# A DiT block's weights in two parts: the low parts of 28 input-weight tiles by a negated copy on ScalarE and an adding transfer

## The chip, the core and the metric

The kernel runs on one core of one Trainium2 chip. The time is device time in microseconds for one execution. Engines: PE is TensorE (PEld its weight loads), DVE is VectorE, ACT is ScalarE, POOL is GpSimd, SP is SyncE, which here only issues DMAs. A line number L234 is line 234 of the kernel before.

## What is computed

Two layers over 256 latent and 256 context tokens of width 1024, all in float32. Each layer is a half FFN, a mixer (attention in the first layer, a bidirectional mLSTM in the second) and another half FFN; every part has its own modulation (shift, scale, gate from a vector per stream) and a post-norm:

```
def half_ffn(h, shift, scale, gate, w_in, w_out, g, b):
    xm = modulate(h, shift, scale)
    a, u = jnp.split(xm @ w_in, 2, axis=-1)
    y = (jax.nn.silu(a) * u) @ w_out
    return post_norm(h, 0.5 * gate * y, g, b)
```

`w_in` is 1024 x 5632 and `w_out` 2816 x 1024. The modulation vectors are `silu(c) @ ada_w[i] + ada_b[i]`, nine chunks of 1024 per layer and stream. There are four half FFNs: the first and second belong to layer 0, the third and fourth to layer 1.

## The kernel before, in words

**Two-part products.** A matmul in full float32 is replaced by three in a reduced form (`fp32r`): each operand is kept as a rounded high part h and the rest, l = x - h, and `mm3` (L232) adds wh*xh, wh*xl and wl*xh in PSUM. Every weight tile is therefore split after it is loaded. `chunk` (L211) does that for a 128 x 1024 tile: `raw` (L197) loads it by a DMA from SP into one of three buffers (`RAW`), `pair` (L206) takes one of seven buffers (`WB`) that hold h and l side by side, and `split` (L217) writes h by a cast on ACT (L218) and l by a subtraction on DVE (L223). The subtraction goes in four pieces while `self.fine` is set. A pair is free again when TensorE has used it, so the cast of a tile waits for TensorE; a raw buffer is free when the subtraction has read it.

**An FFN's order.** `ffn` (L645) works in two halves of 11 hidden units. A unit (`unit_in`, L657) is two weight tiles, 48 matmuls on 512 columns (both token streams together), then the Silu on ACT (L558), the product with the other half on DVE (L559), and a split of the result. Then `unit_out` (L668) multiplies the 11 units by output weights for eight blocks of the width, and the second half follows.

- In the second and third FFN the first half begins with four leading units (`LEAD`), whose weights are kept and used once for the latent and once for the context tokens, while the norm before them is still running. Units 4 to 10 then stream, two tiles each: 14 tiles per FFN, and they are the tiles that the change touches. `fine` is set until unit 6 is emitted.
- Their second halves use another scheme (`fast_in`, L593), which forms sums of weight quarters on DVE; `fast_sums` (L566) makes the sums of the inputs during the output blocks of the first half.
- The first FFN has its own start and no fast half; the fourth has its own function.

**Work on the side.** The modulation vectors of later parts are made on DVE (`ada_dot`, L324 to L327) from tiles of `ada_w` in two buffers (`ada_load`, L317), which SP loads. A few of these products are emitted after each unit (`DOTS`: four behind an input unit, three behind an output block). Each engine works off its own queue in order; the order within a queue comes from a scheduler over the emitted program, apart from instructions that are pinned (`pin`). The residual's scaling (L533 on DVE, L534 on ACT) is emitted behind each unit too. GpSimd does small parts of the norms (L454, L491).

**DMA queues.** All loads are issued from SP. The program reserves 512 bytes per partition for descriptors of transfers that GpSimd issues:

```
nc = _bacc.Bacc("TRN2", target_bir_lowering=False, num_devices=1, dynamic_dma_scratch_size=512)
```

Of the kernel before, what the change touches and what calls it, by code (L numbers as in the profile page):

```python
# [13 lines left out]
AF = mybir.ActivationFunctionType  # L14
ALU = mybir.AluOpType
# [116 lines left out]
def part_k(part, k):  # L132
    return k // 4 * 8 + part * 4 + k % 4


class Stream:


    def __init__(self, b, chunks, sh=0):
        self.b, self.chunks, self.kept = b, chunks, (None, None)  # L140
        self.sh = sh if callable(sh) else lambda c: sh
# [24 lines left out]
class Body:  # L166
    def __init__(self, ctx, tc, a, out):
        self.tc, self.nc, self.a, self.out = tc, tc.nc, a, out
        self.n = 0
        self.sp = ctx.enter_context(tc.tile_pool(name="sp", bufs=1))  # L170
        self.pp = ctx.enter_context(tc.tile_pool(name="pp", bufs=1, space=PSUM))
        self.later, self.running = [], []
        self.fence = {}
        self.fine = False

        self.nraw, self.spare = 0, None


    def t(self, shape, dt=F32, tag=None, bufs=None, pool=None):
# [31 lines left out]
    def chunk(self, src, sh=0):  # L211
        r = self.raw(src)
        h, l = self.pair(sh=sh)
        self.split(r, h, l)
        return h, l

    def split(self, x, h, l):  # L217
# [427 lines left out]
    def ffn(self, layer, s, gate, groups, side, start=None, cpool=None):  # L645
        nc, V = self.nc, self.nc.vector
        li = layer * 2 + s
        allg = BOTH
        call = lambda *k: side.get(k, lambda: None)()
        with self.tc.tile_pool(name=f"ffn{li}", bufs=1) as gp:  # L650
            self.gp, self.gt, self.gw, self.gn = gp, {}, T, NFH
            done = 0
            if start:
                start(self)
                done = NSTART

            def unit_in(j, w, g, steps={}, ks=range(ND), ps=None):  # L657
                n = g[1] - g[0]
                pa, pu = ps or (self.mm(), self.mm())
                for k in ks:  # L660
                    for part, o in ((0, pa), (1, pu)):
                        self.mm3(o[:, :n], w(part_k(part, k)), self.x(k, g), k == 0, k == ND - 1)
                    self.steps(steps.get((j, k), ""))
                if ks[-1] < ND - 1:
                    return pa, pu
                self.ffn_g(j, pa, pu, g)

            def unit_out(hf, d, w, g, steps={}):  # L668
                t0, t1 = g
                y = self.mm()  # L670
                for i in range(NFH):
                    gh, gl = self.gt[hf * NFH + i]
                    self.mm3(y[:, : t1 - t0], w(d * NFH + i), (gh[:, t0:t1], gl[:, t0:t1]), i == 0, i == NFH - 1)
                    self.steps(steps.get((int(g == CTX), d - (ND - TAIL), i), ""))
                for gg in groups:
                    if gg[0] >= t0 and gg[1] <= t1:
                        v = 0 if gg[0] == 0 else 1
                        z = self.h[:, d, gg[0] : gg[1]]
                        V.scalar_tensor_tensor(z, y[:, gg[0] - t0 : gg[1] - t0], gate()[:, v, d : d + 1], z, ALU.mult, ALU.add)  # L679
                        if hf:  # L680
                            self.add_sum(gg, d)

            w_in, w_out = self.a["ffn_in"][li], self.a["ffn_out"][li]
            stream = lambda j: Stream(self, [w_in[2 * j + i] for i in range(2)])
            for hf in range(2):
                js = list(range(hf * NFH, (hf + 1) * NFH))[0 if hf else done :]
                if hf == 0 and not start:
                    first = js[:LEAD]
                    ws = {j: Keep(self, [w_in[2 * j + i] for i in range(2)], SH) for j in first}
                    assert len(self.running) == 1  # L690

                    k0, k1 = range(ND // 2), range(ND // 2, ND)
                    for j in first[:-1]:
                        unit_in(j, ws[j], LAT, LEADSTEP[li])
                    j = first[-1]
                    ps = unit_in(j, ws[j], LAT, ks=k0)
                    assert not self.running
                    pc = unit_in(first[0], ws[first[0]], CTX, ks=k0)
                    ws[j](ND)
                    unit_in(first[0], ws[first[0]], CTX, ks=k1, ps=pc)  # L700
                    unit_in(j, ws[j], LAT, ks=k1, ps=ps)
                    for j in first[1:]:
                        unit_in(j, ws[j], CTX)
                    for j in first:
                        call("in", j)
                    js = js[LEAD:]
                fast = cpool is not None and hf == 1
                for j in js:
                    if fast:
                        self.fast_in(j, w_in, st)  # L710
                        continue
                    unit_in(j, stream(j), allg)
                    assert not self.running
                    if j >= LEAD + FAFTER:
                        self.fine = False
                    call("in", j)
                    self.residual(2, self.pin)
                if not hf:
                    self.residual(len(self.later))
                w = Stream(self, [w_out[hf * NFH + i] for i in range(NFH)])  # L720
                body = ND - TAIL if hf else ND
                if fast:
                    more.close()
                for d in range(body):
                    if cpool and not hf and d == SUMSAT:
                        cpool.close()
                        self.n += 1
                        more = ExitStack()
                        st = more.enter_context(self.tc.tile_pool(name=f"st{self.n}", bufs=1, side="right"))
                        self.fast_operands(st)  # L730
                    unit_out(hf, d, w, allg)
                    if cpool and not hf and d >= SUMSAT and d - SUMSAT < 2:
                        self.fast_sums(d - SUMSAT)
                    call("out", hf, d)
                if body < ND:
                    w = Keep(self, w.chunks, SH, w)
                    self.fine = True
                    for g in groups:
                        for d in range(body, ND):
                            unit_out(hf, d, w, g, TAILSTEP)  # L740
                    self.steps('B')
# [975 lines left out]
```

## Time and profile before

| What | Value |
|---|---|
| Runs (3), median | 1662.06 us (1657.20 to 1662.81) |
| The profiled execution | 1661.01 us, span 1659.1 us |
| Mean granted TensorE clock | 0.992 |
| Busy share PE / PEld / DVE / ACT / POOL | 98% / 88% / 82% / 45% / 4% |
| Read from HBM | 248.76 MB, 151 GB/s over the span |
| Streamed units of the second FFN's first half | about 611 to 687 us |
| Streamed units of the third FFN's first half | about 967 to 1043 us |

Rows of a timeline read: start, length, engine, line, operation, output <- inputs, shapes, count; in brackets the idle time of the engine just before and what ended it. A row of waits reads: who waited, for whom, microseconds in total, times, longest. A row of stretches gives for each engine the busy time and the number of instructions (PE, PEld, DVE, ACT, POOL), then the granted clock, the DMA engines' mean busy share and GB/s. Matmuls are pipelined, so a busy PE is not PE at its peak.

### The profile page before, as it was taken

To read this page: it belongs to the slowest core of one execution; us is meant where nothing else is said; L and a number is where in the kernel's file an instruction comes from. 1 tells how busy PE (TensorE), PEld (TensorE's weight loads), DVE (VectorE), ACT (ScalarE), POOL (GpSimd) and SP (SyncE) were. 2 spreads that over 40 slices of the span, in tenths; PEclk is the share of its full clock that TensorE was granted. 3 is DMA by queue.
4 is the path that set the end of the run, shared out by engine and by line. 5 is a ranking of instruction groups with operands and counts; after the bars stand their busy time and mean duration, and the time that the engine had idled before them with its cause. 6 is when DMAs were issued, how large, how long until landed. Compare 5 with 4: busy or idle time off the path is not lost. (4 is left out here: it accounts for less than half of the span.)

```text
span 1659.1 us, 26570 instructions
## 1 busy us (share of the span) xinstructions
PE 1624.8 (98%) x10308; PEld 1463.5 (88%) x10308; DVE 1354.8 (82%) x2689; ACT 743.6 (45%) x1267; POOL 62.3 (4%) x76
## 2 busy tenths in 40 slices
PE   9999999999989999999999999899999999999998
PEld 6888888899978998889999988689999989999987
DVE  5899977749898979999965888779975967897687
ACT  5532132314765443325652424215651566656542
POOL 0000000001010200000000100000000100020000
PEclk9999999999999999999999999898999999999999
DMA  9577766622203157733352267743351342438552
GB/s 372 188 234 234 246 203 193 200 64 84 64 1 113 54 158 223 218 113 117 113 179 69 84 203 251 256 126 103 127 153 55 111 134 78 128 115 253 179 178 89
DMA packets 72207, 251.54 MB, mean 152 GB/s; under 512 B 7952, under 2 KB 10768, under 8 KB 72080
## 3 DMA queue, kind: packets, MB, share of 16 engines
q1 hardware_dynamic: 71504, 249.05, 47.3%
q8 instruction: 81, 1.33, 0.3%
q10 hardware_dynamic: 576, 0.79, 0.1%
q14 instruction: 46, 0.38, 0.1%
HBM read 248.76 MB, written 1.05 MB: 151 GB/s over the span
## 5 line engine op out<-in xcount | busy, mean ns | idle before, releaser
L234 PE MATMUL t<-t,t 128*128 128x256 f32 (+2 forms) x8412 | 1332.6, 320 | 19.3 <-ACT t L218 15.1
L234 PEld LDWEIGHTS t<-t,t 128*128 128x128 f32 x8412 | 1199.4, 189 | 140.1 <-ACT t L218 17.6
L218 ACT CAST t<-t 128x1024 fp32r<-128x1024 f32 (+3 forms) x521 | 428.4, 843 | 481.7 <-PE t L234 233.4
L223 DVE TENSOR_TENSOR t<-t,t 128x256 fp32r<-128x256 f32 (+2 forms) x740 | 513.6, 728 | 116.9 <-ACT t L218 113.2
L327 DVE SCALAR_TENSOR_TENSOR t<-t,t 128x1024 bf16<-128x1024 f32 x224 | 263.8, 1221 | 28.2 <-DMA t<-in_ada_w 27.3
L894 PE MATMUL t<-t,t 128*128 128x256 f32 (+1 forms) x256 | 79.4, 310 | 0.0
L896 PE MATMUL t<-t,t 128*128 128x256 f32 (+1 forms) x256 | 78.7, 307 | 0.0
L895 PE MATMUL t<-t,t 128*128 128x256 f32 (+1 forms) x256 | 78.4, 306 | 0.0
L558 ACT ACTIVATE t<-t 128x512 f32<-128x512 f32 (+1 forms) x71 | 34.3, 488 | 95.4 <-PE t L234 95.3
L679 DVE SCALAR_TENSOR_TENSOR t<-t,t,t 128x256 f32<-128x256 f32 x96 | 42.6, 478 | 41.6 <-PE t L234 41.6
L559 DVE TENSOR_TENSOR t<-t,t 128x512 f32<-128x512 f32 (+1 forms) x71 | 38.9, 552 | 34.4 <-PE t L234 28.0
L454 POOL TENSOR_TENSOR t<-t,t 128x256 f32<-128x256 f32 x30 | 23.5, 785 | 1142.2 <-ACT t L444 1140.9
L1409 PE MATMUL t<-t,t 128*128 128x512 f32 (+3 forms) x286 | 60.2, 366 | 1.9 <-ACT t L1486 1.0
L822 PE MATMUL t<-t,t 128*128 128x512 f32 (+1 forms) x300 | 60.5, 364 | 0.0
L1409 PEld LDWEIGHTS t<-t,t 128*128 128x128 f32 (+2 forms) x286 | 43.8, 159 | 18.3 <-issue 2.3
L822 PEld LDWEIGHTS t<-t,t 128*128 128x128 f32 x300 | 51.5, 189 | 8.9
L444 ACT ACTIVATE t<-t 128x256 f32<-128x256 f32 x72 | 26.1, 411 | 72.0 <-DVE t L437 72.0
L534 ACT ACTIVATE t<-t,t 128x256 f32<-128x256 f32 x64 | 29.4, 503 | 56.6 <-DVE t L533 56.5
L894 PEld LDWEIGHTS t<-t,t 128*128 128x128 f32 x256 | 48.3, 189 | 2.6
L895 PEld LDWEIGHTS t<-t,t 128*128 128x128 f32 x256 | 48.2, 188 | 2.6
L896 PEld LDWEIGHTS t<-t,t 128*128 128x128 f32 x256 | 48.1, 188 | 2.5
L602 DVE TENSOR_TENSOR t<-t,t 128x512 f32<-128x512 f32 x66 | 45.3, 686 | 0.6
(200 smaller groups left out, 1066.3 us busy)
## 6 DMA issues: line engine op xcount, KB each, us to landing
t<-in_ffn_in SPq DMA_DIRECT2D x168, 512.0 KB, 4.0
t<-in_ada_w SPq DMA_DIRECT2D x137, 512.0 KB, 4.3
t<-in_ffn_out SPq DMA_DIRECT2D x66, 512.0 KB, 4.3
t<-in_ffn_last SPq DMA_DIRECT2D x22, 512.0 KB, 3.6
t<-in_att_in SPq DMA_DIRECT2D x12, 512.0 KB, 3.5
t<-in_att_out SPq DMA_DIRECT2D x8, 512.0 KB, 3.5
t<-in_ml_qk SPq DMA_DIRECT2D x8, 512.0 KB, 3.6
t<-in_ml_v SPq DMA_DIRECT2D x8, 512.0 KB, 3.6
```

The lines of the kernel that those rows point to most:

```text
L218: self.behind(self.nc.scalar.copy(h, x))
L223: self.behind(self.nc.vector.tensor_tensor(out=ls, in0=xs, in1=hs.bitcast(F32), op=ALU.subtract))
L234: mm = lambda *k, **kw: self.nc.tensor.matmul(*k, skip_group_check=not group, **kw)
L327: ins = nc.vector.scalar_tensor_tensor(self.tmp().bitcast(BF16), r, 1.0, self.cb[:, v, :], ALU.mult, ALU.mult, accum_out=to)
L559: V.tensor_tensor(out=sl, in0=sl, in1=pu[:, :n], op=ALU.mult)
L602: add = lambda o, x, y: V.tensor_tensor(out=o, in0=x, in1=y, op=ALU.add)
L679: V.scalar_tensor_tensor(z, y[:, gg[0] - t0 : gg[1] - t0], gate()[:, v, d : d + 1], z, ALU.mult, ALU.add)
L822: pin(nc.tensor.matmul(o, gs[g], ws[k][w][:, i : i + n], start=k == k0 and g == w == 0, stop=k == k1 - 1 and g == 1,))
L894: mm(o, self.xh[:, k, c], wh, start=k == 0, stop=False)
L895: mm(o, self.xh[:, k, c], wl, start=False, stop=False)
L896: mm(o, self.xl[:, k, c], wh, start=False, stop=k == ND - 1)
L1409: mm = lambda *k, **kw: pin(nc.tensor.matmul(*k, **kw))
```

## The change

For the 14 streamed tiles of the second FFN's first half and the 14 of the third's, the low part is made in another way. ACT casts the tile to h as before, then writes the negated tile, rounded to the same reduced form, into l. Then GpSimd issues a DMA that reads the weights from HBM a second time and adds them to what stands in l, which leaves x - h. DVE takes no part. All other splits stay.

```
@@ Body.__init__
+        self.added = False
@@ def chunk(self, src, sh=0):
         r = self.raw(src)
         h, l = self.pair(sh=sh)
-        self.split(r, h, l)
+        if self.added:
+            self.behind(self.nc.scalar.copy(h, r))
+            self.nc.scalar.activation(l, r, AF.Copy, scale=-1.0)
+            self.nc.gpsimd.dma_start(l, src, accum_op=ALU.add)
+        else:
+            self.split(r, h, l)
         return h, l
@@ ffn, for j in js:
+                    self.added = cpool is not None
                     unit_in(j, stream(j), allg)
+                    self.added = False
```

`cpool` is given for the second and third FFN alone, and their second halves leave this loop before these lines.

## The prediction

> **What bounds the kernel now.** I read the page's busy times first, then TensorE's waits, then the two stages that the change touches.
>
> The page's first part:
>
> ```profile
> span 1659.1 us, 26570 instructions
> ...
> PE 1624.8 (98%) x10308; PEld 1463.5 (88%) x10308; DVE 1354.8 (82%) x2689; ACT 743.6 (45%) x1267; POOL 62.3 (4%) x76
> ```
>
> TensorE is busy for 1624.8 of 1659.1 us, so at most 34 us can be won by removing waits alone. The profiled execution took 1661.01 us, 1.05 us below the median of the runs (1662.06), inside their spread of 1657.20 to 1662.81; sums below are made against 1661.0. About 0.3% (5.0 us) is what a measurement of this kernel can tell from no change.
>
> TensorE's own waits (line waited for: us in total, times, longest):
>
> ```profile
> PE t L234 <- ACT t L218: 15.1, 6, 8.2
> PE t L234 <- DVE t L223: 2.0, 4, 1.2
> ```
>
> Half of it is one wait of 8.2 us. The PE timeline and the stretches around it (busy time by engine, granted clock, DMA share, GB/s) show where:
>
> ```profile
> 1059.67 58.63 PE L234 MATMUL t<-t,t 128*128 128x512 f32 x259 [8.20 <-ACT t L218]
> 1119.85 0.39 PE L234 MATMUL t<-t,t 128*128 128x256 f32 x1 [1.55 <-ACT t L218]
> 1120.58 1.44 PE L234 MATMUL t<-t,t 128*128 128x256 f32 x5 [0.35 <-DVE t L223]
> 1124.25 11.03 PE L234 MATMUL t<-t,t 128*128 128x256 f32 x65 [2.23 <-ACT t L218]
> ```
>
> ```profile
> 611.00:687.00 76.00, 76.00 (x337) 62.98 (x336) 72.88 (x123) 25.97 (x38) 0.00 (x0) 1.00 0.73 222
> ...
> 967.00:1043.40 76.40, 76.40 (x341) 63.33 (x340) 66.86 (x112) 24.61 (x35) 0.00 (x0) 1.00 0.77 247
> 1051.50:1059.70 8.20, 0.03 (x1) 0.03 (x1) 5.63 (x9) 1.52 (x3) 0.00 (x0) 0.75 0.84 275
> 1059.70:1065.90 6.20, 6.20 (x15) 4.85 (x16) 4.17 (x8) 0.23 (x1) 0.00 (x0) 0.50 0.80 258
> 1124.30:1130.70 6.40, 6.36 (x28) 6.07 (x29) 5.32 (x6) 3.30 (x6) 0.00 (x0) 0.50 0.41 160
> ```
>
> The two 76 us stretches are the changed units of the second and the third FFN: TensorE has no gap in either, GpSimd (the fifth pair of numbers) does nothing, and the DMA engines are already 0.73 and 0.77 busy. The 8.2 us wait stands behind the third FFN's stretch, at 1051.5; then the clock is granted at 0.50 for 6.2 us, which loses 3.1 us, and 4.1 us of waits (1.55 + 0.35 + 2.23) with 6.4 us at half clock (3.2 us) follow at 1118. So the third FFN holds 8.2 + 3.1 + 4.1 + 3.2 = 18.6 us that are lost to late operands; the second FFN holds nothing.
>
> Why the wait at 1051.5? DVE's timeline through that stage:
>
> ```profile
> 976.75 1.23 DVE L327 SCALAR_TENSOR_TENSOR t<-t,t 128x1024 bf16<-128x1024 f32 x1 [0.95 <-DMA t<-in_ada_w]
> ...
> 982.91 1.22 DVE L327 SCALAR_TENSOR_TENSOR t<-t,t 128x1024 bf16<-128x1024 f32 x1
> ...
> 990.11 1.23 DVE L327 SCALAR_TENSOR_TENSOR t<-t,t 128x1024 bf16<-128x1024 f32 x1 [1.17 <-DMA t<-in_ada_w]
> ...
> 1004.75 1.22 DVE L327 SCALAR_TENSOR_TENSOR t<-t,t 128x1024 bf16<-128x1024 f32 x1
> ...
> 1054.07 1.22 DVE L327 SCALAR_TENSOR_TENSOR t<-t,t 128x1024 bf16<-128x1024 f32 x1 [1.52 <-DMA t<-in_ada_w]
> ...
> 1058.29 0.68 DVE L559 TENSOR_TENSOR t<-t,t 128x512 f32<-128x512 f32 x1
> ```
>
> The last unit's gate product (L559) waits in DVE's queue until 1058.29 behind the modulation products (L327). Those have two load buffers, so a buffer's round is its products plus a reload: SP issues one as soon as the products are done (below, 979.15, for the products at 982.91: 3.76 us). Rounds take (1004.75 - 976.75) / 4 = 7.0 us, and the reload is what most of them wait for, the subtractions only partly.
>
> **Part one: the 28 DVE subtractions that go.** One form per row:
>
> ```profile
> L218 ACT CAST t<-t 128x1024 fp32r<-128x1024 f32 x309 | 322.9, 1050 | 359.5 <-PE t L234 217.2 <-issue 68.0 <-DMA t<-in_ffn_out 23.4
> L223 DVE TENSOR_TENSOR t<-t,t 128x1024 fp32r<-128x1024 f32 x236 | 286.9, 1222 | 67.6 <-ACT t L218 64.8 <-PE t L234 1.5
> L223 DVE TENSOR_TENSOR t<-t,t 128x256 fp32r<-128x256 f32 x350 | 133.8, 426 | 43.0 <-ACT t L218 42.8
> ```
>
> Fourteen tiles per FFN: units 4 to 6 are subtracted in four pieces, 7 to 10 whole. That is 12 x 4 x 0.426 + 16 x 1.222 = 40.0 us of DVE. In the second FFN nothing waits for it, so it is worth 0 there. In the third, two 1.22 us products and a reload of 4.3 us (below) bound a round at 6.7 us, against 7.0 now: over the six rounds between 970 and 1016, some 2 us, at most 3 with the earlier start of the first product.
>
> **Part two: ScalarE.** Its timeline at the first changed tile of each FFN (the cast), and at the Silus of the leading units (L558), behind the last of which TensorE's next work is that tile:
>
> ```profile
> 592.15 1.04 ACT L218 CAST t<-t 128x1024 fp32r<-128x1024 f32 x1
> ...
> 605.25 0.38 ACT L558 ACTIVATE t<-t 128x256 f32<-128x256 f32 x1 [1.41 <-PE t L234]
> ...
> 610.67 0.38 ACT L558 ACTIVATE t<-t 128x256 f32<-128x256 f32 x1 [1.39 <-PE t L234]
> ```
>
> ```profile
> 947.61 1.35 ACT L218 CAST t<-t 128x1024 fp32r<-128x1024 f32 x2
> ...
> 967.10 0.38 ACT L558 ACTIVATE t<-t 128x256 f32<-128x256 f32 x1 [1.48 <-PE t L234]
> ```
>
> 28 negations; no such instruction stands in the trace, the nearest is the cast of the same tile, 1.05 us: 29.4 us. ACT is busy 25.97 of 76.00 us in the stretch, so 14.7 more fit. They are tightest beside the leading units, whose Silus are 610.67 - 605.25 = 5.4 us apart with two tiles between them: 2 x 2.10 + 0.38 + a small cast (1.35 - 1.05 = 0.3 by the row at 947.61) = 4.9 us. I cost it at 0; were that cover gone, it would be 1.05 us per tile, behind which the next cast is queued. The raw buffer is now freed by ACT, not by DVE, so SP's weight loads go out earlier, and in the order of instructions some modulation loads stand one place later on SP.
>
> **Part three: the 28 transfers.** GpSimd has nothing before them and nothing but the next transfer waits behind one in either stretch. But a tile's low half is complete only when its transfer has landed, so TensorE now waits for the DMA, and behind its waiting matmul stand the rest of the in-order stream and the Silu and gate product that follow from it. TensorE's own order stays but for two matmuls. What time there is for that comes out of ACT's rows above.
>
> Second FFN: cast ends at 593.2, negation at 594.2, first use at 610.7. A tile lasts 24 matmuls x 76.00 / 337 = 5.41 us, so the fourteenth is wanted at 610.7 + 13 x 5.41 = 681.0. Third FFN: ready at 950.0, fourteenth wanted at 967.3 + 70.3 = 1037.6. If each transfer takes T and they go one after the other, the fourteenth lands 14 T after the first is ready, and TensorE starts to wait from T = 86.8 / 14 = 6.2 us on (6.26 in the third).
>
> No GpSimd transfer is in the trace. The rows that bound T (queue; then KB each, median us to landing):
>
> ```profile
> q1 hardware_dynamic: 71504, 249.05, 47.3%
> ...
> t<-in_ffn_in SPq DMA_DIRECT2D x168, 512.0 KB, 4.0
> t<-in_ada_w SPq DMA_DIRECT2D x137, 512.0 KB, 4.3
> ...
> t<-in_att_in SPq DMA_DIRECT2D x12, 512.0 KB, 3.5
> ...
> t<-in_start_in SPq DMA_DIRECT2D x1, 512.0 KB, 9.9
> ```
>
> ```profile
> 975.83 0.33 SPq L203 DMA_DIRECT2D t<-in_ffn_in  x1
> 979.15 2.94 SPq L321 DMA_DIRECT2D t<-in_ada_w  x2
> ```
>
> A packet costs an engine 0.473 x 1659.1 x 16 / 71504 = 0.176 us; a 512 KB load is 8 of 4 KB per engine, 1.40 us, so 2.1 of the fastest landing (3.5) are fixed. An accumulation reads the weights and the tile: 16 reads, 2.81 us. Where SP's queue has the engines 0.72 of the time and takes turns, that is 2.81 x 1.72 = 4.8 us. With 2.1 fixed and 0.33 for the issue (SP's row at 975.83; GpSimd's own is not in the trace): **T = 7.3 us**. Bounds: 3.5, if it is no dearer than a plain load on idle engines, and 9.9, the slowest 512 KB load here, in full traffic.
>
> Do they overlap one another? By the Trainium skill, DMA: Bandwidth & Descriptors, section "The descriptor swizzle", a transfer to 128 partitions takes nine read descriptors per engine, and Collectives: The Full Stack, "The bandwidth ceiling", gives an add two reads, so 17; of 16 bytes each, the kernel's 512 bytes of ring hold 32, so an estimate from these pages is that a second one doesn't fit beside the first. No run here shows it. The rows alone lead near: 0.73 busy plus 2.81 / 5.41 = 0.52 is 1.25 of the engines, so even overlapping transfers would only keep a pace of 5.41 x 1.25 = 6.8 us if SP's queue gave nothing up. I take one after the other.
>
> The same DMA page, "Anatomy of one DMA", puts a GpSimd transfer at about 2.0 us plus its bytes at 436 GB/s; for a megabyte read that is an estimate of 4.4 us, by which the sum would be the hidden case below. The rows speak for more, since 1.40 us of transport lands after 4.0 to 4.3 here.
>
> **The sum.** Second FFN: 14 x 7.3 - 86.8 = 15.4 us later. Third FFN: 14 x 7.3 - 87.6 = 14.6 us later, but this fills the 18.6 us that TensorE loses there anyway; what is then late is the modulation chain. Its reloads share the engines: up to 1.4 us more in each of six rounds, +8.4, against the gain of at most 3; I take +2.5, near the middle. Total +17.9: 1661.0 + 17.9 = **1679 us**.
>
> **Rivals.**
> *Transfers far slower* (T 8.5 to 9.9 and above): the loaded row at 9.9 and DVE's 0.96 busy share beside GpSimd speak for it, the unloaded 3.5 against. 28 T - 86.8 - 87.6 - 18.6: +45 at 8.5 (1706), +84 at 9.9 (1745).
> *Hidden* (T under 6.2): 16 us of lead and plain landings of 4.0 to 4.3 speak for it; the double read against. Only the modulation chain is left, -3 to +8: 1658 to 1669, at its middle 1663.5.
> *Faster*: the third FFN's DVE queue sheds its whole subtractions (8 whole tiles x 1.222 = 9.8 us) and the reloads don't lengthen; the gate product comes over 8.2 us earlier, and the wait with its half-clocked 3.1 us goes: 1661.0 - 11.3 = 1649.7. It decides once the modulation loads are not the limit; the waits for `in_ada_w` at 976.75, 990.11 and 1054.07 speak against.
>
> **How the numbers follow.** Moderate wait (T 6.4 to 8.5; 1663 to 1706) 0.50; far slower 0.18; hidden 0.26; faster 0.06. Slower by over 0.3%: 0.95 of the first, all of the second, a quarter of the hidden: 0.72. Same: 0.22. Faster: 0.06. The range reaches from the hidden case's early end, with a little of its spread, 1656, to T = 9.1, 1722; 0.06 lies below and about 0.12 above. The likeliest case's own range is 1663 to 1706.
>
> **What would show it.** Right: GpSimd DMA issues spaced 7 us or so in 594 to 700, and TensorE waiting for a DMA on `in_ffn_in` with waits that appear from about the tenth tile on; 28 ACT instructions of about 1.05 us more; the 8.2 us wait at 1051 smaller or gone. Wrong: no TensorE wait on a DMA in the two stretches (T under 6.2), or waits from the first tile (T over 16); if DVE waits for `in_ada_w` grow beyond 1.4 us a round, the loss is in the modulation chain and not in the weights.

## The result, and the profile after

The changed kernel takes 1700.51 us (median of four runs, 1697.13 to 1706.06) against 1659.63 us for the kernel before (four runs, 1656.26 to 1662.81). The ratio is 1.0246, 95% interval 1.0223 to 1.0269: 40.9 us slower, where 17.9 were forecast. The profiled execution took 1706.06 us, span 1704.0; it is the longest of the four.

The page of the changed kernel (span; busy times; the queue of GpSimd's transfers, with packets, MB and share of 16 engines). Line numbers shift with each edit. In the changed kernel (and in e3, e4, e6, e8, e9 and e13) L216 to L218 are the new cast, negation and transfer, L224 is the cast of all other tiles, L240 the matmul of `mm3`, L333 the modulation product, L565 the gate product. The same cast and matmul are L223 and L239 in e1, L225 and L241 in e5, e7, e11 and e14, L230 and L246 in e2 and e10, and L218 and L234, as before, in e12.

```profile
span 1704.0 us, 26614 instructions
...
PE 1639.8 (96%) x10308; PEld 1468.6 (86%) x10308; DVE 1321.6 (78%) x2625; ACT 769.4 (45%) x1295; POOL 86.8 (5%) x104
...
q0 software_dynamic: 4032, 14.68, 4.9%
```

TensorE's waits in it, and then VectorE's for the modulation loads, in the changed kernel and in the one before:

```profile
PE t L240 <- DMA t<-in_ffn_in: 28.8, 16, 3.8
PE t L240 <- ACT t L224: 15.2, 6, 5.3
```

```profile
DVE t L333 <- DMA t<-in_ada_w: 66.6, 47, 4.3
```

```profile
DVE t L327 <- DMA t<-in_ada_w: 27.3, 36, 2.2
```

TensorE now waits 16 times for a transfer, 28.8 us in all, and VectorE waits 66.6 us for modulation loads, where it waited 27.3. TensorE's timeline shows where:

```profile
635.74 5.76 PE L240 MATMUL t<-t,t 128*128 128x512 f32 x24 [1.76 <-DMA t<-in_ffn_in]
643.58 5.76 PE L240 MATMUL t<-t,t 128*128 128x512 f32 x24 [2.08 <-DMA t<-in_ffn_in]
652.37 12.77 PE L240 MATMUL t<-t,t 128*128 128x512 f32 x48 [3.03 <-DMA t<-in_ffn_in]
...
1101.07 57.06 PE L240 MATMUL t<-t,t 128*128 128x512 f32 x259 [5.31 <-ACT t L224]
1162.67 0.58 PE L240 MATMUL t<-t,t 128*128 128x256 f32 x1 [4.54 <-ACT t L224]
```

Groups of 24 matmuls, one tile each, with a wait in front: TensorE eats a tile and waits for the next. The row at 1101.07 is the old wait of 8.20 us (behind the last unit's gate product), now 5.31. The one at 1162.67 is the old 1.55, now 4.54.

GpSimd's timeline, first and last issue of each FFN:

```profile
595.31 1.02 POOL L218 DMA_DIRECT2D t<-in_ffn_in  x1 [18.62 <-ACT t L224]
...
695.65 0.88 POOL L218 DMA_DIRECT2D t<-in_ffn_in  x1 [6.13 <-ACT t L224]
973.35 0.89 POOL L218 DMA_DIRECT2D t<-in_ffn_in  x1 [19.47 <-PE t L240]
...
1076.44 0.87 POOL L218 DMA_DIRECT2D t<-in_ffn_in  x1 [6.15 <-ACT t L224]
```

Fourteen issues each, so the pace is 100.34 / 13 = 7.72 us and 103.09 / 13 = 7.93 us, where a tile lasts 5.41 us on TensorE. Within each FFN every issue starts 0.26 to 0.32 us after the landing of the transfer before it: they do go one after the other.

The two stretches (engines' busy times, granted clock, DMA share, GB/s); then the DMA issues within the third FFN's (KB each, median us to landing), over 973 to 1084 in the changed kernel and over 970 to 1050 in the one before:

```profile
595.00:703.00 108.00, 93.79 (x462) 77.85 (x460) 69.79 (x124) 47.25 (x66) 12.45 (x14) 0.95 0.93 258
973.00:1084.00 111.00, 96.80 (x467) 79.22 (x466) 59.82 (x108) 44.18 (x59) 12.29 (x14) 0.95 0.92 258
```

```profile
t<-in_ada_w SPq DMA_DIRECT2D x22, 512.0 KB, 5.8
t<-in_ffn_in POOLq DMA_DIRECT2D x14, 512.0 KB, 7.2
```

```profile
t<-in_ada_w SPq DMA_DIRECT2D x25, 512.0 KB, 4.4
```

The DMA engines are 0.93 and 0.92 busy (before, 0.73 and 0.77 in the prediction's stretches, 0.69 and 0.72 over 592 to 687 and 948 to 1043, which begin with the first cast as these do), and a modulation load of the third FFN takes 5.8 us instead of 4.4. VectorE's waits for these loads grew from 9.3 to 31.9 us over the third FFN's two windows.

**Where the time went.** All kernels here run 10308 matmuls in nearly the same order, so the start of the matmul of a given number, less its start in the kernel before, is a delay. The table gives how much the delay grows in each stage (stages by the times of the kernel before; us, worked out from the profiled executions). "Units" is TensorE's work on the changed tiles, "gate" what stands behind the last gate products.

| Kernel | Median, ratio to before [95%] | 2nd FFN units 610–690 | 2nd FFN gate 690–760 | 3rd FFN units 970–1047 | 3rd FFN gate 1047–1085 | 3rd FFN outputs 1085–1145 |
|---|---|---|---|---|---|---|
| changed | 1700.5, 1.0246 [1.0223, 1.0269] | 22.4 | 0.0 | 22.0 | -4.4 | 2.2 |
| e1 no transfer | 1660.2, 0.9997 [0.9988, 1.0007] | 0.0 | 0.0 | 0.0 | -0.3 | -0.8 |
| e2 traffic only | 1693.8, 1.0199 [1.0184, 1.0214] | 1.9 | 12.0 | 0.1 | 13.0 | -1.0 |
| e3 second FFN | 1686.1, 1.0156 [1.0131, 1.0181] | 22.4 | 0.0 | 0.0 | -0.4 | -1.0 |
| e4 third FFN | 1676.9, 1.0108 [1.0087, 1.0129] | 0.0 | 0.0 | 18.3 | -6.3 | -0.5 |
| e5 wait only | 1700.0, 1.0239 [1.0198, 1.0281] | 28.5 | 0.0 | 27.1 | -9.4 | 1.7 |
| e6 plain transfer | 1667.6, 1.0043 [1.0030, 1.0056] | 0.0 | 1.8 | 0.0 | 3.3 | -0.4 |
| e7 every second | 1680.1, 1.0117 [1.0089, 1.0145] | 0.0 | 8.8 | 0.0 | 12.1 | -0.3 |
| e8 ring 2048 | 1696.9, 1.0222 [1.0189, 1.0256] | 11.0 | 3.3 | 9.1 | 7.2 | -0.6 |
| e9 ring, third buffer | 1675.0, 1.0078 [1.0062, 1.0095] | 6.0 | 2.9 | 3.0 | 8.0 | -4.2 |
| e10 plain traffic only | 1679.2, 1.0099 [1.0078, 1.0120] | 0.1 | 6.1 | 0.1 | 6.1 | -1.2 |
| e11 short wait | 1660.0, 1.0000 [0.9989, 1.0012] | 0.0 | 0.0 | 0.0 | -0.9 | -0.6 |
| e12 before, third buffer | 1644.0, 0.9896 [0.9881, 0.9910] | 0.0 | 0.0 | 0.0 | -11.4 | -3.9 |
| e13 change, third buffer | 1693.5, 1.0186 [1.0148, 1.0224] | 25.7 | 0.0 | 28.4 | -11.4 | -8.7 |
| e14 second tile, third buffer | 1652.0, 0.9942 [0.9926, 0.9959] | 0.0 | 0.0 | 0.0 | -2.8 | -8.7 |

The medians of before that belong to these runs lie between 1659.6 and 1661.8. The change's own row: 22.4 + 22.0 - 4.4 + 2.2 = 42.2 us of the 45 by which the two profiled executions differ; the stages left out hold the rest. Two kernels that do nothing new in a stage differ there by about 1 us (e3 in the third FFN: -0.4 and -1.0).

### The profile page after: what moved, and what is told of

It is laid out like the page before. It is cut to its first block, busy times and chain, and to the rows that moved or that the text cites. A ratio compares the mean times of both kernels' runs of the same rounds, so it can differ in the third digit from the quotient of the medians.

```text
span 1704.0 us, 26614 instructions
## 1 busy us (share of the span) xinstructions
PE 1639.8 (96%) x10308; PEld 1468.6 (86%) x10308; DVE 1321.6 (78%) x2625; ACT 769.4 (45%) x1295; POOL 86.8 (5%) x104
## 3 DMA queue, kind: packets, MB, share of 16 engines
q0 software_dynamic: 4032, 14.68, 4.9%
## 5 line engine op out<-in xcount | busy, mean ns | idle before, releaser
L240 PE MATMUL t<-t,t 128*128 128x256 f32 (+2 forms) x8412 | 1346.9, 321 | 48.1 <-DMA t<-in_ffn_in 28.8
L240 PEld LDWEIGHTS t<-t,t 128*128 128x128 f32 x8412 | 1204.5, 190 | 178.2 <-DMA t<-in_ffn_in 36.0
L224 ACT CAST t<-t 128x1024 fp32r<-128x1024 f32 (+4 forms) x493 | 399.4, 831 | 457.7 <-PE t L240 207.2
L229 DVE TENSOR_TENSOR t<-t,t 128x256 fp32r<-128x256 f32 (+3 forms) x676 | 478.4, 738 | 120.2 <-ACT t L224 116.0
L333 DVE SCALAR_TENSOR_TENSOR t<-t,t 128x1024 bf16<-128x1024 f32 x224 | 264.0, 1220 | 67.1 <-DMA t<-in_ada_w 66.6
L565 DVE TENSOR_TENSOR t<-t,t 128x512 f32<-128x512 f32 (+1 forms) x71 | 38.9, 552 | 68.2 <-PE t L240 40.4
L450 ACT ACTIVATE t<-t 128x256 f32<-128x256 f32 x72 | 26.1, 411 | 71.6 <-DVE t L443 71.6
```

What stands on the lines that cost most here:

```text
L224: self.behind(self.nc.scalar.copy(h, x))
L229: self.behind(self.nc.vector.tensor_tensor(out=ls, in0=xs, in1=hs.bitcast(F32), op=ALU.subtract))
L240: mm = lambda *k, **kw: self.nc.tensor.matmul(*k, skip_group_check=not group, **kw)
L333: ins = nc.vector.scalar_tensor_tensor(self.tmp().bitcast(BF16), r, 1.0, self.cb[:, v, :], ALU.mult, ALU.mult, accum_out=to)
L565: V.tensor_tensor(out=sl, in0=sl, in1=pu[:, :n], op=ALU.mult)
```

## The experiments

**e1: what is the rest worth without the transfers?**

```
-            self.nc.gpsimd.dma_start(l, src, accum_op=ALU.add)
```

> The changed kernel without its 28 transfers: ScalarE still writes the negated tile, VectorE still does not subtract, nothing is added (the low parts are wrong by the missing addend). It prices the change's other two parts alone. If the whole loss of the change lies in the transfers (their time, or their traffic), this runs at 1648 to 1660 us: at most the 11.3 us of the prediction's rival 'faster' below before, and no more than before. If the 28 negations on ScalarE or the new release of the raw buffers cost something, it is above before by what they cost, up to 28 x 1.05 = 29 us.

1660.18 us, ratio 0.9997 [0.9988, 1.0007]. So the whole loss lies in the transfers. VectorE's 40 us of relief bring 1.1 us in the third FFN (-0.3 - 0.8), no more than e3 shows there without any, and nothing in the second: TensorE's wait behind the gate product is as long as before. What VectorE no longer subtracts it spends in part waiting for modulation loads, 36.2 us over the run instead of 27.3. TensorE's waits in this run:

```profile
PE t L239 <- ACT t L223: 15.5, 6, 8.7
```

**e2: the traffic without the wait.** A tile `d` of its own takes the transfers.

```
+            self.split(r, h, l)
+            k = self.t([P, 1], tag="tok", bufs=6)
+            self.nc.scalar.copy(k, r[:, :1])
...
+            self.nc.gpsimd.tensor_copy(d[:, :1], k)
+            self.nc.gpsimd.dma_start(d, src, accum_op=ALU.add)
```

> The kernel before, with VectorE's subtractions kept, plus the same 28 adding transfers of 512 KB into a tile that nobody reads; each is released by a 4-byte-wide copy of ScalarE that follows the tile's cast, so they start when those of the change start. TensorE never waits for them. Two theories for the third FFN's 19 us. Contention (the second reading and the adding lengthen the modulation loads, whoever waits): VectorE's waits for in_ada_w grow by some 35 to 40 us as in the changed kernel, the third FFN ends 15 to 19 us later, the time is 1673 to 1680. Coupling (the modulation loads stand in SP's queue behind weight loads, and those behind TensorE, which waits for transfers): without TensorE's waits the rounds stay near 7.0 us, and the time is within 4 us of before, 1657 to 1664.

1693.81 us, above both expectations. Some 4 us of it have gathered by 610, most of them before the first transfer, and are not explained; most of the rest has its place at the gates, 12.0 us in the second FFN and 13.0 in the third. TensorE's timeline, and the modulation loads' landing over 954 to 1070:

```profile
706.92 0.79 PE L246 MATMUL t<-t,t 128*128 128x512 f32 x1 [6.80 <-ACT t L230]
...
1080.92 0.80 PE L246 MATMUL t<-t,t 128*128 128x512 f32 x1 [11.77 <-ACT t L230]
...
1092.81 7.47 PE L246 MATMUL t<-t,t 128*128 128x512 f32 x25 [7.45 <-ACT t L230]
```

```profile
t<-in_ada_w SPq DMA_DIRECT2D x20, 512.0 KB, 5.9
```

The second FFN, which had no wait before, now has one of 6.80 us, and the third's 8.20 has become 11.77 and 7.45. TensorE doesn't wait for these transfers: they lengthen the modulation loads (5.9 us, as in the changed kernel), and the gate product stands behind their products. VectorE's waits for the modulation loads grew by 9.8 us around the second FFN's units and gate and by 8.3 around the third's. Contention is shown; the coupling through SP's queue isn't needed for it. But the edit is not as clean as its expectation has it: in the trace the small copies don't follow their tiles' casts, they wait in ScalarE's queue for the weight loads (35.5 and 32.2 us around the two FFNs), ahead of other casts and of Silus, and the first transfer starts at 589.35, before its tile is cast. VectorE's waits for casts and Silus grew by 1.6 us in the second FFN and 5.2 in the third. So the 25.0 us at the gates are an upper bound for the price of the traffic.

**e3 and e4: one FFN at a time.**

```
-                    self.added = cpool is not None
+                    self.added = li == 1        # e4: li == 2
```

> The change in the second FFN alone (14 tiles). From the two traces this FFN was later by 23 us, 14.6 us of it waits for the transfers and the rest half-clocked matmuls: 1660 + 23 = 1683, with nothing in the third FFN. If part of the loss in the third FFN is what the second handed on (modulation vectors that came late, a lower clock), it is higher than 1683, up to 1700; if the second FFN's delay is made good later, lower.

> The change in the third FFN alone (14 tiles). By the prediction's step (the waits fill what is lost there anyway) +2.5 us, 1662. By the trace of the changed kernel +19 us, 1679. If the two FFNs add up, this and the run for the second FFN together give the 40.9 us of the whole change.

1686.10 and 1676.90 us. By the stages the second FFN costs 22.4 and the third 18.3 - 6.3 - 0.5 = 11.5; the medians say 25.5 and 16.3, together 41.9 against the change's 40.9. The medians add up, and nothing is seen to be handed on. Both profiled executions are the fastest of their four, so the medians lie above the stages. The expectation of 19 for the third was some 3 us too high by the medians.

**e5: the wait without the traffic.** Two transfers of 4 KB in place of one of 512.

```
-            self.nc.gpsimd.dma_start(l, src, accum_op=ALU.add)
+            for i in range(2):
+                self.nc.gpsimd.dma_start(l[:, :8], src[:, :8], accum_op=ALU.add)
```

> The changed kernel with each 512 KB transfer replaced by two adding transfers of 8 columns (4 KB) of the same tile, one behind the other (the rest of the low part lacks the addend): a serial wait with next to no traffic. Its length per tile is not known; two issues of 0.9 us and two landings of 2 to 3 us make 5 to 8 us. The prediction's formula for the second FFN, 14 T - 86.8, is tried without contention: at T up to 6.2 no loss, 1660; at 7.5, 18 us of waits plus about half as much of half-clocked matmuls there. If the third FFN's loss of the change is due to the traffic, here its waits are paid back by the old 8.2 us wait and its half clock (up to 11.3 us): at T 7.5 the third FFN loses 8 us or less more than that; if it is due to the order on SP's queue, it loses as much as the second.

1700.03 us: as much as the change, with next to no bytes. TensorE's waits, its timeline behind the last unit, and the issues over 977 to 1093:

```profile
PE t L241 <- DMA t<-in_ffn_in: 37.5, 19, 5.5
```

```profile
1106.72 55.77 PE L241 MATMUL t<-t,t 128*128 128x512 f32 x259 [1.70 <-ACT t L225]
```

```profile
t<-in_ada_w SPq DMA_DIRECT2D x24, 512.0 KB, 4.6
...
t<-in_ffn_in POOLq DMA_DIRECT2D x28, 4.0 KB, 3.9
```

The pairs are issued 8.1 and 8.3 us apart. The modulation loads land in 4.6 us, nearly as before, and the old 8.20 us wait shrinks to 1.70: 9.4 us are paid back at the gate, against 4.4 in the changed kernel. That is the prediction's step "the waits fill what is lost there", without contention. Of the 18.6 us that it counted on, 9.4 - 1.7 = 7.7 came back. VectorE's waits for modulation loads did not grow here (7.2 us over 977 to 1093; 9.3 over 970 to 1050 in the kernel before), so TensorE's waits alone don't delay these loads through SP's queue. And the half-clocked matmuls that the expectation put on top of the formula don't come on top: at the measured pace the formula gives 26.8 us, and the units take 28.5.

**e6: plain transfers.**

```
-            self.nc.gpsimd.dma_start(l, src, accum_op=ALU.add)
+            self.nc.gpsimd.dma_start(l, src)
```

> The changed kernel with plain transfers in place of adding ones (the addend replaces the negated tile, so the low part is wrong): the same issue by GpSimd and the same wait, one read instead of two. If the second read makes the price, the transfer lands in 4 to 5 us, TensorE doesn't wait for it, and with the engines' share at about 0.99 instead of over 1 the modulation chain is a few us later: 1660 to 1672. If the price is in GpSimd's way of issuing (serial, with its own descriptors), the transfer still takes about 7 us and the time stays near 1700.

1667.59 us, as the first theory had it, and TensorE waits for no transfer. The queue and the issues of its transfers, GpSimd's group, and four of its issues:

```profile
q0 software_dynamic: 4032, 14.68, 2.6%
...
t<-in_ffn_in POOLq DMA_DIRECT2D x28, 512.0 KB, 5.2
```

```profile
L218 POOL DMA_DIRECT2D t<-in_ffn_in x28 | 15.1, 540 | 157.2 <-ACT t L217 110.8 <-PE t L240 27.7 <-ACT t L224 18.6
```

```profile
599.28 0.53 POOL L218 DMA_DIRECT2D t<-in_ffn_in  x1 [4.43 <-ACT t L217]
602.30 0.53 POOL L218 DMA_DIRECT2D t<-in_ffn_in  x1 [2.49 <-ACT t L217]
604.83 0.54 POOL L218 DMA_DIRECT2D t<-in_ffn_in  x1 [2.00 <-PE t L240]
607.85 0.53 POOL L218 DMA_DIRECT2D t<-in_ffn_in  x1 [2.49 <-PE t L240]
```

A packet takes 0.026 x 1665.3 x 16 / 4032 = 0.17 us; the adding one 0.049 x 1704.0 x 16 / 4032 = 0.33. Adding doubles the engines' time per byte, adds 0.34 us to the issue (0.54 against 0.88) and 2.2 us to the landing. The plain transfers differ in a second way, which the expectation did not have: issued 2.5 to 3.0 us apart at 5.2 us each, they overlap with the same 512 bytes of descriptors. How much of the vanished wait each of the two took away, the shorter transfer or the overlap, was not separated.

**e7: one tile of two.**

```
-        if self.added:
+        self.nadd += self.added
+        if self.added and self.nadd % 2:
```

> The change in one of the two tiles of each unit, 14 of 28 in all: a transfer has 10.8 us in place of 5.4, more than the 7.4 that it takes, so TensorE should not wait for it, and the added traffic is halved (0.73 + 0.26 of the engines' time). If both costs are thresholds (pace against transfer time, engines at their limit), nearly all of the loss goes: 1660 to 1666. If traffic costs in proportion, half of the 33 us of the run with traffic alone stays: 1676.

1680.10 us. TensorE waits for no transfer, as both theories had it, but 8.8 and 12.1 us are lost at the gates. The traffic's price is no threshold, and it falls by less than the bytes do: half of them cost 20.9 us, all of them without a wait 25.0 at most (12.0 + 13.0, e2). The time is 4 us above the 1676 of the second theory.

**e8: several transfers in flight.**

```
-dynamic_dma_scratch_size=512
+dynamic_dma_scratch_size=2048      # and five instead of six buffers "tmp"
```

> The changed kernel with 2048 instead of 512 bytes per partition for GpSimd's descriptors (and five instead of six buffers of VectorE's temporary tile, to make room). If the transfers go one after the other only because the descriptors of a second one don't fit, issues now come 5.4 us apart, several are in flight, and TensorE's waits for transfers go: 1675 to 1690, the traffic's cost left. If the DMA engines are the limit (0.9 to 0.96 busy with the transfers), the pace stays at 6.5 to 7.5 us, each transfer only takes longer from issue to landing, and the time stays at 1693 to 1708.

1696.90 us. GpSimd's issues in the second FFN, the transfers' landing, and TensorE's waits:

```profile
593.18 1.02 POOL L218 DMA_DIRECT2D t<-in_ffn_in  x1 [18.89 <-ACT t L224]
...
669.93 0.86 POOL L218 DMA_DIRECT2D t<-in_ffn_in  x1 [6.73 <-ACT t L217]
```

```profile
t<-in_ffn_in POOLq DMA_DIRECT2D x28, 512.0 KB, 8.6
```

```profile
PE t L240 <- ACT t L224: 23.4, 9, 8.3
PE t L240 <- DVE t L565: 10.9, 2, 5.6
```

Issues are 5.90 us apart on average while each transfer takes 8.6, so they overlap, and no wait of TensorE for a transfer is left: with 512 bytes it was the room for descriptors that kept them one after the other. The mechanism is the first theory's, at nearly TensorE's pace, and the time the second's: the wait went and the loss stayed. What TensorE waits for now is the gate product L565 (two waits, 10.9 us) and the casts behind it.

**e9: the larger ring and a third modulation buffer.**

```
-        r = self.t([P, 1024], tag="ada", bufs=2, pool=self.cp)
+        r = self.t([P, 1024], tag="ada", bufs=3, pool=self.cp)
```

> The kernel with 2048 bytes of descriptors and a third load buffer for the modulation tiles (three instead of two). In the run with 2048 bytes TensorE no longer waited for transfers, and the 37 us were lost behind gate products that stand behind the modulation products. If that chain's loss is the latency of its reloads (a buffer's round is its products plus a reload, which the traffic lengthens), a third buffer takes most of it away: 1660 to 1675. If it is the engines' throughput (no more bytes get through, however many loads are out), the third buffer changes nothing: 1690 to 1700.

1674.96 us, the upper end of the first theory; but most of the 21.9 us below e8 is what a third buffer brings without the change too (16, e12). Over the kernel before with the same buffers the change still loses 31 us, against 37 with two: with 28 adding transfers in flight, room for one more load hides little. The number is the first theory's; by this comparison the second is nearer.

**e10: plain traffic only** (e2 with plain transfers).

> The run with traffic alone again, with plain transfers into the tile that nobody reads in place of adding ones; VectorE's subtractions are kept. The plain transfer of the changed kernel cost 6 us, the adding one without anybody waiting 33 us, but the first had VectorE relieved of 28 subtractions and the second had not. If the adding makes the difference, this is near 1667; if VectorE's relief does, it is near 1685.

1679.24 us, between the two expectations: by the stages 6.1 + 6.1 = 12.2 us at the gates (and 3.1 before 610, as in e2), where e2's adding traffic cost 25.0 and e6 with VectorE relieved 1.8 + 3.3 = 5.1. So the adding costs 13 us. The other 7 us are at most what VectorE's relief is worth on loaded engines, where e1 shows none on quiet ones: e10 also has e2's small copies, and e6 does not.

**e11: a short wait** (e5 with one transfer of 4 KB).

> The run with waits alone again, with one adding transfer of 8 columns per tile in place of two (the rest of the low part lacks the addend). One took 3.7 us from issue to landing, so with its issue a pace of about 4 us, under the 5.4 us that TensorE takes for a tile. By the threshold of the prediction no wait is seen and the time is 1657 to 1662. If any serial wait behind GpSimd costs something per tile whatever its length, it is above 1670.

1660.04 us, ratio 1.0000 [0.9989, 1.0012]: TensorE waits for no transfer. These go one after the other too, every 4.7 to 4.8 us on average; a serial transfer under TensorE's 5.41 us is free here.

**e12: the third modulation buffer in the kernel before** (e9's edit alone).

> The kernel before with a third load buffer for the modulation tiles and nothing else. In the third FFN the gate products come 12.0 us apart where TensorE needs 10.8 us for a unit, held by the modulation products in front of them. If reload latency is what holds these, the 8.2 us wait at 1051 and its half clock go: 1645 to 1653, faster than both kernels. If it is VectorE's own work or the engines' throughput, the time stays within 3 us of before.

1644.03 us, ratio 0.9896 [0.9881, 0.9910]: faster than both kernels, a little below the first theory's range. TensorE's largest waits, and its timeline through the third FFN:

```profile
PE t L234 <- ACT t L218: 3.1, 3, 1.8
```

```profile
935.80 170.55 PE L234 MATMUL t<-t,t 128*128 128x256 f32 x900
1107.35 3.11 PE L234 MATMUL t<-t,t 128*128 128x256 f32 x24 [0.99 <-ACT t L627]
```

From 935.8 to 1106.4 TensorE has no gap: the wait of 8.20 us and its half clock are gone, with the same bytes and the same work on VectorE. It was the latency of the reloads.

**e13 and e14: the change with the third buffer**, whole, and in one tile of two (e7 and e9's edits). They were run to see how the two costs share the loss.

> The changed kernel with a third load buffer for the modulation tiles, and with 512 bytes of descriptors as it was. The transfers still go one after the other, at 7.7 to 7.9 us each, so both FFNs are held to 14 times that: 14 x 7.7 - 86.8 and 14 x 7.9 - 87.6 make some 21 to 23 us each. Nothing is there to be given back, since the third buffer alone already took the old waits away: 1644 + 44 = 1688. If the modulation chain and the waits add up in the changed kernel rather than stand in for one another, it gains all that the kernel before gained, 16 us, and is at 1685 or below; if it is the faster of the two that is hidden, it gains only the third FFN's part, 1690 to 1700.

> The change in one tile of each unit (14 of 28) with a third load buffer for the modulation tiles. TensorE waited for no transfer with every second tile, and its 20 us were lost behind the modulation products. If that loss is the length of their reloads, three buffers hide it and the time is that of the kernel before with three buffers plus a little: 1644 to 1652. If the engines have no room for the bytes, as the run with the larger ring and three buffers (1675, 31 us above 1644 with all 28 tiles) suggests, half of that stays: 1660.

1693.52 and 1651.97 us. TensorE's waits in e13, and in e14:

```profile
PE t L240 <- DMA t<-in_ffn_in: 35.7, 15, 4.4
```

```profile
PE t L241 <- ACT t L225: 8.8, 4, 5.7
```

With the third buffer the change gains some 7 us where the kernel before gains 16; e13's runs reach from 1684.70 to 1699.12, so the 7 is rough, and the 1688 of its first sum is not excluded. The median is in the range of the last theory, but that theory did not have the reason. By the profiled executions: the chain's relief comes in full (gate and outputs of the third FFN fall from -4.4 + 2.2 to -11.4 - 8.7, by 17.9 us), and the transfers give 9.7 of it back (25.7 + 28.4 instead of 22.4 + 22.0 in the units), since they are now issued 8.02 and 8.26 us apart. That the modulation loads, three at a time, are what slows them was only argued. In e14, where nobody waits for a transfer, three buffers hide most of the traffic: 8 us are left over e12, the upper end of the first theory.

## Why the prediction was wrong

**Right.** The bottleneck, and the mechanism of the second FFN: transfers go one after the other and TensorE waits for their pace. 28 negations of 1053 ns, 29.5 us in all, cost nothing, and 40 us less of VectorE's work is worth nothing that can be told (e1). The changed kernel's groups:

```profile
L217 ACT ACTIVATE t<-t 128x1024 fp32r<-128x1024 f32 x28 | 29.5, 1053 | 0.0
L218 POOL DMA_DIRECT2D t<-in_ffn_in x28 | 24.7, 884 | 218.5 <-issue 69.9 <-ACT t L224 52.5 <-PE t L240 33.0
```

The formula holds too, within 3 us. With the measured pace p, 14 p - 86.8 (87.6 in the third) against the delay of the units: changed kernel 21.3 and 23.4 for 22.4 and 22.0; e3 25.2 for 22.4; e4 (7.44) 16.6 for 18.3; e5 26.8 and 28.6 for 28.5 and 27.1; e13 25.5 and 28.1 for 25.7 and 28.4. It holds though it has no term for the matmuls at half clock (clock 0.95 over the stretches): the transfers set the end, so time lost at half clock is taken off the next wait. And the runs fit its threshold: at a pace under 5.41 (e11) nothing waits.

**First step that failed: the size of T.** T was 4.8 for the bytes + 2.1 fixed + 0.33 for the issue = 7.3; measured are 7.72 and 7.93. The terms were further off than their sum. Transfers of 4 KB, one after the other, come every 4.06 and 4.15 us (half of e5's 8.1 and 8.3), so about 4.1 us are not bytes, where 2.1 + 0.33 = 2.43 were set; the issue alone takes 0.88 (row above) and not SP's 0.33. That leaves 7.72 - 4.06 = 3.7 us for the bytes, not 4.8 (an estimate, as e5's engines are less busy). That one term too small and one too large came within 0.4 to 0.6 us of the measured paces together is luck. What was missing is taken 14 times: 22.4 instead of 15.4 us in the second FFN, and 22.0 instead of 14.6 in the third.

**Second step that failed: "this fills the 18.6 us that TensorE loses there anyway".** Measured at the gate and in the outputs, only 4.4 - 2.2 = 2.2 us came back. Two things were wrong in it. The 7.3 us at 1118 were not filled by an earlier wait: they stayed, or grew by up to 2.2, in every kernel with two modulation buffers (last column, -1.2 to 2.2). And of the 11.3 us at the gate, 9.4 come back where the transfers have next to no bytes (e5), but 4.4 where they have (6.3 in e4): the modulation loads land in 5.8 us instead of 4.4. The bound of 1.4 us a reload was met by these medians; its effect was priced at +2.5 us, near the middle, where traffic alone costs up to 13.0 us at that gate (e2). The third FFN came to 22.0 - 4.4 + 2.2 = 19.8 us, not 2.5.

Together (22.4 - 15.4) + (19.8 - 2.5) = 24.3 us, which is 42.2 - 17.9. The second step is the larger: with the measured paces the prediction's own sum would have been 21.3 + (23.4 - 18.6) = 26.1 us, 28.6 with its +2.5 for the chain; the rest is time that did not come back. The measured time lies within the likeliest case's 1663 to 1706, but that case reaches so far only by a T of 8.5, which was not the reason.

**What was not seen.** The second FFN has a modulation chain too. It was taken to hold nothing because no wait stood there; without a wait for transfers the same traffic costs 12.0 us at its gate (e2), and half of it 8.8 (e7). In the changed kernel this column is 0.0; the reading is that the waits for transfers give the chain the time that it lacks, and e8, where those waits go and waits for the gate product come, fits it. So taking away either cost alone helps little: without the bytes 1700 (e5; its pace was some 0.4 us longer, which makes 11.2 us in the units, so an estimate of 1689 at the change's pace), without the wait 1694 (e2) and 1697 (e8). The two alone, by this some 29 us and 33, come to more than the 40.9 of both.

**The rivals.** "Hidden" fell with the pace of 7.7 us. "Faster" wanted 11.3 us from VectorE's relief; without any transfer it brought 1.1 at most (e1), so the wait at 1051 was never VectorE's subtractions but the reloads (e12). "Far slower" would have needed T of 8.5 and more; each issue took 0.86 to 1.02 us, so nothing shows VectorE holding GpSimd up.

**Signs.** Issues 7 us apart, waits on `in_ffn_in`, 28 more ACT instructions and a smaller wait at 1051 came as foretold. The first wait came at the fifth tile in the second FFN and the fourth in the third, not "about the tenth": by the prediction's own numbers the first transfer leaves 610.7 - 594.2 - 7.3 = 9.2 us and each further tile takes 7.3 - 5.41 = 1.9 of them, so the sixth would have followed. One sign of being wrong came too: VectorE's waits for `in_ada_w` grew by 31.9 - 9.3 = 22.6 us over the third FFN's 22 loads, some 2 us for each round of two, beyond the 1.4 that was named. The prediction put that as a loss in the chain and not in the weights; both were there.

**Descriptors and landing.** The trace agrees with the estimate drawn from the Trainium skill, DMA: Bandwidth & Descriptors, "The descriptor swizzle", with Collectives: The Full Stack, "The bandwidth ceiling", that a second adding transfer doesn't fit into 512 bytes: with 512 each issue follows a landing, 7.7 us apart, with 2048 they are 5.9 us apart at 8.6 us each. "Anatomy of one DMA", in the same DMA: Bandwidth & Descriptors of the Trainium skill, gave an estimate of 4.4 us for a transfer; 7.4 was measured beside SP's loads, and 3.7 to 4.0 for one of 4 KB, for which its formula gives an estimate of about 2.0.

**Open.** Why half of the adding transfers (e7) cost 20.9 us at the gates where all as plain ones with as much engine time (14 x 8 x 0.17 = 19 us an FFN, 7 x 8 x 0.33 = 18) cost 5.1 (e6): part may be VectorE's relief (e10), the rest was not separated. The modulation loads don't tell it: they land in 4.6 us in both over 594 to 690, and in 5.1 against 4.7 over 960 to 1050. What the wait at 1118 hangs on, beyond that it is shorter with a third buffer, was not tried.

## What to carry to other kernels

A serial helper is priced by its pace, issue included, against the pace of the engine that eats its results; under it is free (e11), over it every tile pays the whole difference once the lead (here 610.7 - 594.2 = 16.5 us) is used up. Before traffic is added to a stage, look for the chain there whose loads have the fewest buffers, even where no wait shows it yet: here that chain, without the wait, cost about as much as the wait did, and a third buffer for it made the kernel before 1.0% faster. Where two costs partly stand in for one another, what removing one brings is not its price.

## What the runs showed of the hardware

An adding DMA from GpSimd takes 0.88 us to issue (a plain one 0.54, SP's 0.33) and twice the engine time per packet (0.33 against 0.17 us). One that adds 4 KB lands after 3.7 to 4.0 us, one that adds 512 KB after 7.4, counted from the start of the issue, so about half of the time is not bytes. With 512 bytes for descriptors adding transfers go one at a time, the next issue 0.26 to 0.32 us after a landing, while plain ones overlap (e6). With 2048 bytes the adding ones overlap too, and each then takes longer (8.6 us) while the modulation loads beside them take 6.4 (e8, over 963 to 1048).
